# Two-layer trunk on one core: the state product takes one summed operand, and the instruction order is drawn up from other costs

## Chip, cores and metric

The kernel runs on one core of a Trainium2 chip. The time is the device time of one execution in microseconds. TensorE is the matrix engine; VectorE, ScalarE and GpSimd are the other compute engines, and SyncE (SP) issues most transfers. In the profile they are PE (with PEld for its weight loads), DVE, ACT, POOL and SP.

## What is computed

Two residual layers over 256 positions of width 1024, in float32. The first is a state-space mixer, the second an attention:

```python
for i in range(DEPTH):                    # DEPTH = 2
    hn = rms_norm(h, norm_g[i])
    y = s5_mixer(hn, ...) if i % 2 == 0 else moba_mixer(hn, ...)
    h = h + y
# s5_mixer: u, z = split(hn @ w_in); 64 groups of 16 channels and 64 complex states
#   s[t] = a * s[t-1] + f * (B u[t]);  y = Re(C s) + d * u
#   y = gelu(y); y = y * sigmoid(y @ w_glu + b_glu); return (y * silu(z)) @ w_out
# moba_mixer: q, k, v, z = split(hn @ w_in); 8 heads of 128, norm and rotation of q and k
#   causal attention over the one block of 256 keys; return (o * silu(z)) @ w_out
```

## The kernel before

**How the order comes about.** Every engine call is recorded in `add` as an operation with its engine, an estimated cost, and the operations that it has to follow (data, and the reuse of a buffer: a tile with `bufs=n` goes round among n places). Several calls inside `prog.group()` are one operation. `lay` then plays all five engines forward with those costs: whichever engine is free next takes, among its ready operations, the one with the longest remaining way to the end. `order` does so for some rounds, keeps the best way lengths, and the start times of the last pass are the order in which instructions are written out. So each engine's instruction list is fixed ahead of the run, and a wrong cost can put a waiting instruction in front of ready ones. All instructions are issued from one helper line, L355 in the profile, so groups are told apart by tile names.

**Stages.** (1) Eight `u_step`s multiply the rows of x with the first half of the input weights, 512 columns in plain float32 (each such multiplication is two instructions of TensorE). Their order on TensorE is fixed, with `x_turn8` (transposes of x) and `b_turn` among them; `c_turn` (16 transposes of the output matrix C, from the buffer `Y`) is placed freely, with a push of 10000. (2) The states. For each quarter b of 16 groups VectorE makes an input table `X[b]` (`x_table`: six multiplications and additions of 128x512, buffer `X`, three places), and an output table in `Y` (`y_table`). TensorE turns `X[b]` (`x_turn`) and multiplies it with C (`k_table`); from the four results `w_table` makes `W` (buffer `BW`). `ssm_in(b)` brings the input into states; `rotate(b)` on VectorE multiplies with cosines and sines (`EC`, `ES`) into `t1` and `t2` (two places each) and scans along time; `states(b)` rotates back and leaves two addends, `pa` (tile `tb`, two places) and `pc` (tile `t3`; the profile calls t1, t2 and t3 all `t`). `ssm_within(b)` opens the accumulation of the output with `W`, and `ssm_out(b)` adds the product of `Y` with `pa` and then with `pc`, 32 matrix products of 64x64 by 64 for each. ScalarE takes the result out (`ys`), four transposes and a GELU follow. `z_pair` (64 products of 256 columns in all, from tiles `zh` and `zl`) is independent of all that and fills TensorE in between. (3) `glu_tile`: eight output tiles in split precision (`hi` and `lo` parts, three products each), the parts made by ScalarE and VectorE from each weight tile `wr`. (4) The first output product. (5) The attention: six `chunk`s for q, k and v, normed in `qk_chunk` with a power on GpSimd (tiles `sm`, `mhalf`), eight `head`s, the gate and the last output product.

**The transpose of `b_glu`** (`vb`, a part of the same buffer `Y`) stands in the free part behind `c_turn`; the new contents of `Y` have to follow it.

Of the kernel before, what the change touches and what calls it, by code (L numbers as in the profile page):

```python
# [20 lines left out]
F = mybir.dt.float32  # L21
# [50 lines left out]
class Op:  # L72
    __slots__ = ("eng", "calls", "cost", "deps", "nbytes", "i", "table", "columns", "parts", "push", "mode")


class Program:
# [67 lines left out]
    def add(self, handle, eng, method, a, k):  # L144
# [9 lines left out]
        if dma:  # L154
            cost = self.ISSUE[eng]
        elif eng == "PE":
            if method == "transpose":
                cost = 109 if aps[0].shape[0] >= 64 else 30
            else:
                m, c = n(aps[0]), n(aps[1])  # L160
                if aps[0].dtype == FR:
                    cost = 4 + 0.4455 * max(c, 256)
                else:
                    cost = max(4 * c / 2.4 + 2, 109) * m / 128 * aps[0].shape[0] / 128
                    if m == 32:
                        cost = 42
        elif eng == "DVE":
            two = method in ("tensor_tensor", "scalar_tensor_tensor", "tensor_tensor_scan", "tensor_reduce") or psum
            cost = (70 if not psum else 125) + n(aps[0] if method == "tensor_reduce" else out) * (6.4 if method == "reciprocal" else 2.1 if method == "tensor_tensor_scan" else 1.04 if two else 0.53)
        elif eng == "ACT":  # L170
            cost = 95 + 0.83 * n(aps[0]) + (60 if len(aps) > 1 else 0) + (100 if "accum_out" in k else 0)
        else:
            spread = any(not x.ap[-1][0] for x in aps)
            each = {"memset": 0.85, "tensor_scalar": 5.2}.get(method, 1.8 if spread else 2.2)
            cost = 150 + 205 * n(out) if k.get("op") == OP.pow else 60 + n(out) * each
        if self.open is None:
            op = Op()
            op.eng, op.calls, op.cost, op.deps, op.i = eng, [], 0, {}, len(self.ops)
            op.nbytes, op.table, op.columns, op.parts, op.push, op.mode = 0, None, 0, [], self.push, None
# [5 lines left out]
            if dma and eng == "SP" and self.behind is not None:  # L185
                op.deps[self.behind] = -1
            if self.open is not False and self.grouping:
                self.open = op
        else:
            op = self.open  # L190
        op.calls.append((handle, method, a, k))
        op.cost += cost
        if eng == "PE":
            rows, m = aps[0].shape[0], n(aps[0])
            cycles = 2 * rows if method == "transpose" else n(aps[1]) * (1 if aps[0].dtype == FR else 4)
            first = int(aps[0].offset) // int(np.prod(aps[0].tensor.shape[1:]))
            op.mode = rows <= 64, m <= 64
            op.parts.append((first, rows, max(1, 128 // m), cycles * rows / 128))

            op.columns = sum(w / min(side, sum(q[:2] == (f, r) for q in op.parts)) for f, r, side, w in op.parts)  # L200
# [3 lines left out]
        if dma:  # L204
# [26 lines left out]
    grouping, chain, only, behind, push = False, None, None, None, 0  # L231
# [26 lines left out]
    def lay(self, after, way, forth):  # L258
# [10 lines left out]
        table, columns, mode = None, {}, None  # L269
        for _ in ops:  # L270
# [13 lines left out]
            if e == "PE" and forth:  # L284
                left_over, at = cost, t
                while left_over > 0:
                    tick = int(at // TICK)
                    pace = 1 if columns.get(tick - 1, 0) >= BUSY else 2
                    part = min(left_over, ((tick + 1) * TICK - at) / pace + 1e-6)
                    columns[tick] = columns.get(tick, 0) + o.columns * part / cost  # L290
                    left_over -= part
                    at += part * pace
                cost = at - t
            if o.nbytes and e != "POOL":
                t = max(t, hwdge)
                hwdge = t + 480 * len(o.calls)
# [61 lines left out]
RATE = 270  # L358
MODE = 3000
# [5 lines left out]
NUDGES = ()  # L365
# [10 lines left out]
YZ_G = True  # L376
# [8 lines left out]
def body(ctx: ExitStack, tc: tile.TileContext, x, norm_g, w_in1, a_re, a_im, log_dt, b_re, b_im,  # L385
# [41 lines left out]
    plan = []  # L427
# [26 lines left out]
    state = {"load": 0, "split": 16}  # L454
    AHEAD = 4
# [7 lines left out]
    def load_to(n):  # L463
        while state["load"] < min(n, len(plan)):
# [5 lines left out]
            if len(src.ap) == 3:  # L470
                dst = dst.rearrange("p (k n) -> p k n", k=src.ap[1][1])
            SP.dma_start(dst, src)

    def split_part(i, c0, c1):
# [5 lines left out]
        hi, lo = (w[:, c0:c1] for w in whl[i])  # L480
        act(hi, raw[i][:, c0:c1])
        tt(V, lo, raw[i][:, c0:c1], hi.bitcast(F), SUB)
# [101 lines left out]
    V.tensor_copy(vec[:, 0:16], pt[:, 256:272])  # L584
    xT = tile_([128, 8, S], F, name="ah")
# [230 lines left out]
    def k_table(b):  # L816

        p = wide()
        xv = X[b].rearrange("p (r q x) -> p r q x", r=2, q=8)
        with prog.group():  # L820
            for r in range(2):
                for a in range(2):
                    for hh in range(4):
                        for j2 in range(2):
                            o = 512 * j2 + 16 * hh
                            PE.matmul(p[side(a), o:o + 16], xv[side(j2), r, 2 * hh + a], ct_[side(j2), r, 8 * b + 2 * hh + a],
                                      start=(r == 0 and hh == 0), stop=(r == 1), skip_group_check=True)
        kv = lambda t: t[:, 8 * b:8 * b + 8].rearrange("p (h j) c -> p h j c", j=2)
        tt(V, kv(KS), p.rearrange("p (j x) -> p j x", j=2)[:, :, 0:64].rearrange("p j (h c) -> p h j c", c=16), kv(dm), ADD)

    def w_table():
# [3 lines left out]
        for t in (2, 1, 0):  # L835
            ps = [acc(), acc()]
            with prog.group():
                for a in range(2):
                    rows, o = side(a), C_ID + 64 * a + 16 * (3 - t)
                    PE.matmul(ps[a][rows], cst[rows, o:o + 64], kv[rows], start=True, stop=True)  # L840
            for a in range(2):
# [5 lines left out]
    def ssm_in(b):  # L847

        p = wide()
        prog.push = 10000  # L850
# [8 lines left out]
        prog.push = 0  # L859
# [26 lines left out]
    def states(b, t2, p):  # L886
# [10 lines left out]
        tt(V, gm(pc)[:, 1, :, 1:], z[:, 0], es, MUL)  # L897
        PSTS[b] = pa, pc
# [11 lines left out]
    def ssm_within(b):  # L910
# [6 lines left out]
        prog.push = 20000  # L917
# [5 lines left out]
        prog.push = 0  # L923
        return p

    def ssm_out(b, p):
        for i, t in enumerate(PSTS[b]):
            tv = t.rearrange("p (r a h m) -> p r a h m", r=2, a=2, h=4)
            with prog.group():
                for r in range(2):  # L930
                    for h in range(4):
                        for a in range(2):
                            for j2 in range(2):
                                product(p, h, a, j2, tv[side(j2), r, a, h],
                                        Y[side(j2), r, 8 * b + 2 * h + a].rearrange("p k c -> p (k c)"), False, i == 1 and r == 1)
# [14 lines left out]
    def z_pair(m):  # L950
# [9 lines left out]
        act(zz[:, 2 * m:2 * m + 2].rearrange("p a (m s) -> p a s m", s=4), p.rearrange("p (a s m) -> p a s m", a=2, s=4), AF.Silu)  # L960


    with prog.fixed("PE"):
        for k in range(8):
# [3 lines left out]
            if k == 1:  # L968
                b_turn()
    load_to(14)  # L970
    prog.push = 10000
    c_turn()
    prog.push = 0
    pv0 = wide()
    PE.transpose(pv0[:, 0:8], vb, ident[32:40, 32:40])
    V.tensor_copy(vec[:, 16:24], pv0[:, 0:8])
# [65 lines left out]
    for n in range(8):  # L1042
        if YZ_G:
            tt(V, yT[:, n], yT[:, n], zz[:, n], MUL)
        else:
            stt(V, yT[:, n], yT[:, n], 0.5, zz[:, n], MUL, MUL)
# [275 lines left out]
```

## Time and profile before

| what | value |
|---|---|
| median of 3 runs | 293.67 us (291.27 to 294.46) |
| the profiled execution | 293.73 us |
| its span, first to last instruction | 291.9 us |
| TensorE matmul busy, of the span | 280.2 us, 2551 instructions |
| TensorE weight loads busy | 229.0 us, 2551 instructions |
| VectorE busy | 214.9 us, 430 instructions |
| ScalarE busy | 159.1 us, 306 instructions |
| GpSimd busy | 22.7 us, 26 instructions |

The span leaves out 1.8 us that lie around it. Busy times of one engine are shares of the same span. Neighbouring matmuls overlap in the records, so what one takes of TensorE is read from start to start.

### The profile page before, as it was taken

The numbers are of one execution on the slowest core, as the hardware profiler recorded it, in microseconds if no ns is written. First come the engines' busy times: TensorE is split into PE (matmuls) and PEld (weight loads), VectorE is DVE, ScalarE is ACT, GpSimd is POOL, SyncE is SP. The second block draws the span as 40 slices with busy tenths as digits, with TensorE's granted clock in tenths as the row PEclk, the third lists the DMA queues.
The fourth block names the chain that finished last, engine by engine and source line by source line (L and its number), as shares of the span: only waits on it lengthen the run. The fifth ranks groups of instructions, "written<-read, shape, count | busy, mean of one in ns | idle before, by whom it ended". The sixth has DMA issues, their size and how long they took to land.

```text
span 291.9 us, 6324 instructions
## 1 busy us (share of the span) xinstructions
PE 280.2 (96%) x2551; PEld 229.0 (78%) x2551; DVE 214.9 (74%) x430; ACT 159.1 (55%) x306; POOL 22.7 (8%) x26
## 2 busy tenths in 40 slices
PE   8998999999998969999999999899999999999995
PEld 7454458888677859998888888678888799998884
DVE  0959789998958647976439648898679988699603
ACT  2579347377440358766429347557565766585300
POOL 3100013000000000000000014500013100000000
PEclk9999999999999988999999999999999999999999
DMA  5999454882000193876745643565245472434003
GB/s 177 244 331 277 126 161 122 213 227 76 0 2 2 39 271 131 240 216 207 212 137 153 209 149 138 165 201 187 96 138 162 136 214 77 144 120 166 6 0 144
DMA packets 41596, 43.91 MB, mean 150 GB/s; under 512 B 4552, under 2 KB 31136, under 8 KB 41504
## 3 DMA queue, kind: packets, MB, share of 16 engines
q1 hardware_dynamic: 40608, 42.68, 50.2%
q10 hardware_dynamic: 864, 0.82, 0.8%
q8 instruction: 20, 0.33, 0.5%
q14 instruction: 8, 0.07, 0.1%
q0 software_dynamic: 96, 0.02, 0.0%
HBM read 41.41 MB, written 1.05 MB: 145 GB/s over the span
## 4 chain that ended last, share of the span: by engine, by line
PE 73%; DVE 7%; DMA 6%; ACT 5%; issue 4%; POOL 3%; SPq 1%; ACTq 0%; POOLq 0%
PE uz L355 33%; PE acc L355 23%; PE wide L355 17%; DMA zz<-in_x_dram 4%; POOL sm L355 3%; DVE sm L355 2%; DMA wr<-in_attn_w_in_dram 2%; DVE D L355 2%; ACT ES L355 1%; SPq L355 1%; DVE xp L355 1%; DVE zl L355 1%; ACT EC L355 1%; DVE X L355 1%; ACT X L355 1%
## 5 line engine op out<-in xcount | busy, mean ns | idle before, releaser
L355 DVE TENSOR_TENSOR xp<-wr,X 128x1024 fp32r<-128x1024 f32 x28 | 34.0, 1222 | 13.8 <-ACT X L355 13.7
L355 DVE TENSOR_TENSOR zl<-wr,zh 128x1024 fp32r<-128x1024 f32 x28 | 34.1, 1219 | 6.6 <-ACT zh L355 6.5
L355 ACT ACTIVATE zh<-wr 128x1024 fp32r<-128x1024 f32 x28 | 29.4, 1056 | 15.7 <-PE uz L355 7.9
L355 ACT ACTIVATE X<-wr 128x1024 fp32r<-128x1024 f32 x28 | 29.5, 1057 | 14.7 <-PE uz L355 8.1
L355 PE MATMUL uz<-al,zh 128*128 128x256 f32 x96 | 24.5, 349 | 0.0
L355 PEld LDWEIGHTS uz<-al,zh 128*128 128x128 f32 x96 | 17.9, 190 | 2.7 <-issue 0.8
L355 POOL TENSOR_TENSOR sm<-sm,mhalf 128x4 f32<-128x4 f32 x8 | 13.7, 1714 | 50.7 <-DVE sm L355 50.6
L355 PE MATMUL uz<-zh,ah 128*128 128x512 f32 x40 | 17.6, 490 | 0.0
L355 PE MATMUL acc<-zh,ah 128*128 128x512 f32 x40 | 17.6, 484 | 0.0
L355 PE MATMUL uz<-zl,ah 128*128 128x512 f32 x40 | 17.1, 478 | 0.0
L355 PE MATMUL acc<-zl,ah 128*128 128x512 f32 x40 | 17.1, 476 | 0.0
L355 PE MATMUL uz<-al,zl 128*128 128x256 f32 x64 | 16.6, 389 | 0.0
L355 PEld LDWEIGHTS uz<-al,zl 128*128 128x128 f32 x64 | 11.4, 190 | 3.0 <-issue 1.6
L355 DVE TENSOR_TENSOR Y<-acc,Y 128x512 f32<-128x512 f32 x4 | 2.8, 691 | 11.4 <-PE acc L355 11.4
L355 PEld LDWEIGHTS acc<-zl,ah 128*128 128x128 f32 x40 | 7.5, 189 | 4.2 <-issue 3.3
L355 DVE TENSOR_TENSOR tb<-s,yT 128x512 f32<-128x512 f32 x16 | 10.7, 682 | 0.0
L355 ACT ACTIVATE ys<-acc 128x256 f32<-128x256 f32 (+1 forms) x8 | 3.8, 496 | 12.4 <-PE acc L355 12.3
L355 PEld LDWEIGHTS acc<-zh,ah 128*128 128x128 f32 x40 | 7.4, 190 | 3.9 <-issue 2.9
L355 PEld LDWEIGHTS uz<-zl,ah 128*128 128x128 f32 x40 | 7.3, 189 | 3.3 <-issue 2.2
L355 PEld LDWEIGHTS uz<-zh,ah 128*128 128x128 f32 x40 | 7.3, 189 | 3.3 <-issue 2.4
L355 PE MATMUL uz<-X,ah 128*128 128x512 f32 x24 | 9.9, 411 | 0.0
L355 PE MATMUL acc<-X,ah 128*128 128x512 f32 x24 | 9.8, 408 | 0.0
(279 smaller groups left out, 804.8 us busy)
## 6 DMA issues: line engine op xcount, KB each, us to landing
wr<-in_attn_w_in_dram SPq DMA_DIRECT2D x32, 512.0 KB, 4.2
zl<-in_ssm_w_in_dram SPq DMA_DIRECT2D x8, 512.0 KB, 6.8
wr<-in_ssm_w_glu_dram SPq DMA_DIRECT2D x8, 512.0 KB, 6.3
wr<-in_ssm_w_out_dram SPq DMA_DIRECT2D x8, 512.0 KB, 4.3
wr<-in_attn_w_out_dram SPq DMA_DIRECT2D x8, 512.0 KB, 4.3
zh<-in_ssm_w_in_dram SPq DMA_DIRECT2D x7, 512.0 KB, 8.4
zz<-zz SPq DMA_DIRECT2D x8, 128.0 KB, 2.3
Y<-in_x_dram SPq DMA_DIRECT2D x2, 512.0 KB, 5.2
```

What stands on the lines that cost most here:

```text
L355: getattr(handle, method)(*map(self.real, a), **{q: self.real(v) for q, v in k.items()})
```

## The change

The products of `ssm_out` take one operand in place of two: `pa + pc` is formed on VectorE for all four quarters. `X[3]` is placed in `t1`. The transpose of `b_glu` is written ahead of the u steps, and `c_turn` stands in the fixed order of TensorE behind `u_step(5)`. The costs from which the order is drawn up are others: SiLU, GELU, the power on GpSimd, and the small products of TensorE get set lengths (41 ns each in `k_table`, 500 in `w_table`, 31 in `ssm_in`, 32 in `ssm_within`, 31 in `ssm_out`), and the player of the order counts TensorE's instructions in pages of 256, with a time from the moment that a page is asked for until it is there. Eleven random disturbances of the way lengths (`NUDGES`) are applied before the last pass. What else the diff brings (`EARLY`, `LOW_DMA`, `HOLD`, `Z_TANH`) is switched off by its constants.

```diff
-                    if m == 32:
-                        cost = 42
+                    if self.unit:
+                        cost = self.unit
...
-            cost = 95 + 0.83 * n(aps[0]) + (60 if len(aps) > 1 else 0) + (100 if "accum_out" in k else 0)
+            f = a[2] if len(a) > 2 else AF.Copy
+            each = {AF.Silu: 1.57, AF.Gelu_apprx_tanh: 1.36}.get(f, 0.83)
+            cost = 95 + each * n(aps[0]) + (60 if len(aps) > 1 else 0) + (100 if "accum_out" in k else 0)
...
-            cost = 150 + 205 * n(out) if k.get("op") == OP.pow else 60 + n(out) * each
+            cost = 700 + 350 * n(out) if k.get("op") == OP.pow else 60 + n(out) * each
...
+            op.words += 2 if method == "transpose" or aps[0].dtype == FR else 4
...
+        words, landed = 64, {0: 0.0, 1: 0.0}
...
+                page, to = words // 256, words + o.words
+                if (to + 48) // 256 > (words + 48) // 256:
+                    at = t + cost * (((to + 48) // 256 * 256 - 48 - words) / o.words)
+                    landed[(to + 48) // 256 + 1] = at + (3500 if dma < at + 1500 else 6000)
+                if to // 256 > page:
+                    cost += max(0.0, landed.get(page + 1, 0.0) - t - cost * ((page + 1) * 256 - words) / o.words)
+                words = to
...
+EARLY = {}
+XT1 = 3
+HOLD = False
+Z_TANH = ()
+YZ_G = not Z_TANH
+CT = 5
+LOW_DMA = ()
+SUM = (0, 1, 2, 3)
...
-NUDGES = ()
+NUDGES = (1046, 1100, 1127, 1187, 1265, 1346, 1586, 2485, 2533, 2578, 2604)
...
+    PE.transpose(pt[:, 272:280], vb, ident[32:40, 32:40])
+    V.tensor_copy(vec[:, 16:24], pt[:, 272:280])
...
-        X[b] = tmp("X", NX)
+        X[b] = tmp("t1", 2) if b == XT1 else tmp("X", NX)
...
+        prog.unit = 41
...
+                prog.unit = 500
...
+        prog.push, prog.unit = 10000, 31
...
+        prog.push, prog.unit = 20000, 32
...
+        if b in SUM:
+            tt(V, pa, pa, pc, ADD)
+            pc = None
         PSTS[b] = pa, pc
...
-        for i, t in enumerate(PSTS[b]):
-            tv = t.rearrange("p (r a h m) -> p r a h m", r=2, a=2, h=4)
+        parts_ = [t.rearrange("p (r a h m) -> p r a h m", r=2, a=2, h=4) for t in PSTS[b] if t is not None]
+        prog.unit = 31
+        for tv in parts_:
...
+            if k == CT:
+                c_turn()
     load_to(14)
-    prog.push = 10000
-    c_turn()
-    prog.push = 0
...
-    PE.transpose(pv0[:, 0:8], vb, ident[32:40, 32:40])
-    V.tensor_copy(vec[:, 16:24], pv0[:, 0:8])
```

## Rows read from the trace of the kernel before

**Rows 1.** Busy time of each engine in stretches of the span: from and to in us, length, then for each engine busy us and instructions, the granted clock of TensorE (1.00 is full), the busy share of the 16 transfer engines and GB/s.

```profile
28.00:44.00 16.00, 15.85 (x66) 8.51 (x67) 13.11 (x23) 6.39 (x13) 1.08 (x1) 1.00 0.58 156
44.00:104.50 60.50, 59.02 (x1332) 49.19 (x1330) 52.00 (x76) 30.50 (x52) 3.00 (x4) 1.00 0.35 92
104.50:107.40 2.90, 0.01 (x2) 0.00 (x0) 1.63 (x6) 1.28 (x4) 0.00 (x0) 1.00 1.02 284
107.40:111.00 3.60, 3.58 (x18) 3.24 (x19) 0.00 (x0) 2.17 (x6) 0.00 (x0) 0.53 0.93 296
111.00:135.00 24.00, 24.00 (x196) 23.71 (x197) 19.35 (x34) 17.66 (x33) 0.00 (x0) 1.00 0.64 194
180.00:192.00 12.00, 10.63 (x54) 8.09 (x53) 10.80 (x25) 6.75 (x9) 5.30 (x2) 1.00 0.51 160
192.00:291.90 99.90, 96.28 (x590) 84.56 (x588) 73.14 (x168) 53.23 (x112) 5.28 (x4) 1.00 0.41 127
```

**Rows 2.** The chain of work that ended last, 82 to 112 us, in order of time: start us, length us, what; "issue" is time in which the engine waited for nothing that the profile shows.

```profile
93.65 0.94 issue
...
104.51 2.92 issue
107.42 0.33 PE wide L355 x3
```

**Rows 3.** TensorE's instructions in order of time, 90 to 95 us and 101 to 108 us: start us, length us, line, operation, output<-inputs, shapes, count, idle time before.

```profile
90.41 1.16 PE L355 MATMUL acc<-Y,tb 64*64 64x64 f32 x64
91.39 1.11 PE L355 MATMUL acc<-Y,t 64*64 64x64 f32 x64
92.32 1.11 PE L355 MATMUL wide<-Y,tb 64*64 64x64 f32 x64
...
102.47 1.11 PE L355 MATMUL wide<-Y,tb 64*64 64x64 f32 x64
103.41 1.10 PE L355 MATMUL wide<-Y,t 64*64 64x64 f32 x61
```

**Rows 4.** The transfer queues in the stretch 104 to 108 us: queue and kind, packets, MB, share; "instruction" packets carry instructions to an engine.

```profile
q1 hardware_dynamic: 2162, 1.09, 101.8%
q8 instruction: 1, 0.02, 1.9%
```

**Rows 5.** TensorE's instructions in order of time, 24 to 30 us, in the middle of the fifth u step.

```profile
25.27 1.88 PE L355 MATMUL uz<-zh,ah 128*128 128x512 f32 x4
28.15 1.21 PE L355 MATMUL wide<-cst,Y 64*128 64x64 f32 x16 [1.00 <-ACT ah L355]
```

**Rows 6.** VectorE's waits from 20 to 112 us: what it was about to do, what it waited for, us in total, how many, the longest.

```profile
DVE al L355 <- ACT ah L355: 5.8, 2, 4.5
DVE tb L355 <- PE acc L355: 5.3, 3, 3.0
DVE vec L355 <- PE wide L355: 2.8, 1, 2.8
DVE Y L355 <- PE wide L355: 1.7, 2, 1.3
...
DVE X L355 <- PE wide L355: 0.4, 1, 0.4
```

**Rows 7.** Groups of VectorE's instructions from 20 to 112 us by shape: count, busy us and mean ns of one, idle before.

```profile
L355 DVE TENSOR_TENSOR al<-ah,rrow 128x1024 f32<-128x1024 f32 x2 | 2.4, 1217 | 0.0
```

**Rows 8.** VectorE's instructions in order of time at the transposed `b_glu`, at `X[3]`, at the second rotation, and around the last two `states`: the `TENSOR_SCALAR` rows write the first column of `pa` once TensorE has run `ssm_within`.

```profile
37.58 0.17 DVE L355 COPY vec<-wide 128x8 f32<-128x8 f32 x1 [2.76 <-PE wide L355]
...
46.13 1.66 DVE L355 TENSOR_TENSOR X<-s,yT 128x512 f32<-128x512 f32 x2 [0.41 <-PE wide L355]
...
65.87 1.21 DVE L355 TENSOR_TENSOR t<-wide,EC 128x1024 f32<-128x1024 f32 x1
...
91.64 1.21 DVE L355 TENSOR_TENSOR tb<-t,EC 128x1008 f32<-128x1008 f32 x1 [0.81 <-PE acc L355]
...
96.60 0.19 DVE L355 TENSOR_SCALAR tb<-acc 128x16 f32<-128x16 f32 x1 [1.45 <-PE acc L355]
...
98.75 0.19 DVE L355 TENSOR_SCALAR tb<-wide 128x16 f32<-128x16 f32 x1 [0.79 <-PE wide L355]
```

**Rows 9.** TensorE's instructions in order of time, 64 to 73 us: the last `k_table`.

```profile
69.19 1.27 PE L355 MATMUL wide<-yT,X 64*64 64x16 f32 x58
```

**Rows 10.** TensorE's waits in the whole span: what it was about to do, what it waited for, us in total, how many, the longest.

```profile
PE wide L355 <- issue: 3.9, 2, 2.9
PE wide L355 <- DVE D L355: 1.4, 3, 0.7
...
PE wide L355 <- ACT ah L355: 1.0, 1, 1.0
PE wide L355 <- DVE Y L355: 0.3, 1, 0.3
PE acc L355 <- DVE vec L355: 0.3, 1, 0.3
PE uz L355 <- ACT um L355: 0.2, 1, 0.2
```

**Rows 11.** The chain that ended last from 174 to 192 us: the power on GpSimd in the norm of q and k.

```profile
174.11 1.02 POOL sm L355
...
184.84 3.19 POOL sm L355
```

More of the change, by code (lines that the diff above doesn't have):

```diff
@@ L72 @@
 class Op:
-    __slots__ = ("eng", "calls", "cost", "deps", "nbytes", "i", "table", "columns", "parts", "push", "mode")
+    __slots__ = ("words", "eng", "calls", "cost", "deps", "nbytes", "i", "table", "columns", "parts", "push", "mode")
 class Program:
@@ L184, in add @@
                 self.chain[eng] = op.i
-            if dma and eng == "SP" and self.behind is not None:
-                op.deps[self.behind] = -1
+            if dma and eng == "SP":
+                for j in (self.behind, self.late):
+                    if j is not None:
+                        op.deps[j] = -1
             if self.open is not False and self.grouping:
@@ L203, in add @@
             op.table = {AF.Silu: 0, AF.Sin: 0, AF.Gelu_apprx_tanh: 1, AF.Exp: 2}.get(f)
-        if dma:
+        if dma and "accum_op" in k:
+            op.nbytes = int(np.prod(out.shape)) * 8
+        elif dma:
             run = out.ap[-1][1] if len(aps[0].ap) > 1 else 1
@@ L230, in add @@
             self.seen[name] = keep
-    grouping, chain, only, behind, push = False, None, None, None, 0
+    grouping, chain, only, behind, push, unit, late = False, None, None, None, 0, 0, None
     @contextmanager
@@ L375 @@
 EV_G = ()
-YZ_G = True
 YL_G = ()
@@ L454, in body @@
     state = {"load": 0, "split": 16}
+    last_out = []
     AHEAD = 4
@@ L471, in load_to @@
                 dst = dst.rearrange("p (k n) -> p k n", k=src.ap[1][1])
+            prog.late = last_out[0] if i >= 20 and last_out else None
             SP.dma_start(dst, src)
+            prog.late = None
     def split_part(i, c0, c1):
@@ L480, in split_part @@
         hi, lo = (w[:, c0:c1] for w in whl[i])
+        prog.push = EARLY.get(i, 0)
         act(hi, raw[i][:, c0:c1])
-        tt(V, lo, raw[i][:, c0:c1], hi.bitcast(F), SUB)
+        if i in LOW_DMA:
+            act(lo, hi.bitcast(F), AF.Copy, scale=-1.0)
+            G.dma_start(lo.rearrange("p (k n) -> p k n", k=8), plan[i], accum_op=ADD)
+        else:
+            tt(V, lo, raw[i][:, c0:c1], hi.bitcast(F), SUB)
+        prog.push = 0
     def split_to(n):
@@ L840, in w_table @@
                     PE.matmul(ps[a][rows], cst[rows, o:o + 64], kv[rows], start=True, stop=True)
+            prog.unit = 0
             for a in range(2):
@@ L934, in ssm_out @@
                                 product(p, h, a, j2, tv[side(j2), r, a, h],
-                                        Y[side(j2), r, 8 * b + 2 * h + a].rearrange("p k c -> p (k c)"), False, i == 1 and r == 1)
+                                        Y[side(j2), r, 8 * b + 2 * h + a].rearrange("p k c -> p (k c)"), False,
+                                        tv is parts_[-1] and r == 1)
+        if HOLD:
+            last_out[:] = [len(prog.ops) - 1]
+        prog.unit = 0
         ys = tile_([128, 4, 8, 16], F, name="ys", bufs=2)
@@ L959, in z_pair @@
                           start=(k == 0), stop=(k == 7))
-        act(zz[:, 2 * m:2 * m + 2].rearrange("p a (m s) -> p a s m", s=4), p.rearrange("p (a s m) -> p a s m", a=2, s=4), AF.Silu)
+        zo, zi = zz[:, 2 * m:2 * m + 2].rearrange("p a (m s) -> p a s m", s=4), p.rearrange("p (a s m) -> p a s m", a=2, s=4)
+        if m in Z_TANH:
+            for q in range(2):
+                act(zo[:, q], zi[:, q], AF.Tanh, scale=0.5)
+                stt(V, zo[:, q], zo[:, q], 1.0, zi[:, q], ADD, MUL)
+        else:
+            act(zo, zi, AF.Silu)
     with prog.fixed("PE"):
@@ L969, in body @@
                 b_turn()
+            if k == CT:
+                c_turn()
     load_to(14)
-    prog.push = 10000
-    c_turn()
-    prog.push = 0
+    if CT > 7:
+        prog.push = 10000
+        c_turn()
+        prog.push = 0
     pv0 = wide()
-    PE.transpose(pv0[:, 0:8], vb, ident[32:40, 32:40])
-    V.tensor_copy(vec[:, 16:24], pv0[:, 0:8])
     for i in range(2):
```

9 lines of the change are left out of this document (5 added, 4 removed).

## Prediction, made before the changed kernel was run

> **What bounds the kernel now.** I read the stretches first [rows 1]. From 111 us to the end TensorE's busy time fills nearly every stretch (24.00 of 24.00, 96.28 of 99.90, of which the last 3.3 us are the way out), and the exception, 180 to 192 us, lacks 1.4 us. So the second half is bound by TensorE, and nothing there is taken away. The state stage, 44 to 104.5 us, is busy for 59.02 of 60.50 on TensorE and for 52.00 on VectorE: TensorE bounds it, VectorE is close behind. Right after it come 2.90 us in which TensorE does nothing, and 3.60 us in which it is busy with a granted clock of 0.53, that is mostly at the lower of its two levels, 1.2 GHz. Then the chain [rows 2]: the stage's two holes, 0.94 and 2.92 us, are put down to "issue", so no engine and no data is named. The waits of TensorE [rows 10] show that all others together (1.4, 1.0, 0.3, 0.3, 0.2 us) are smaller than these 3.9. Last, TensorE's order in time [rows 3] shows where the holes stand: inside `ssm_out`, in the run of 64x64 products from `t`, the second addend.
>
> That the holes are instructions that have not arrived is an inference. For it: they cut one group of like instructions in two, and in the window of the longer one the queue that carries instructions moved one packet while ordinary transfers filled the transfer engines (101.8%) [rows 4].
>
> **The change, part by part.** All is counted against the profiled execution, 293.73 us (291.9 of span and 1.8 around it), which stands at the median of the three runs, 293.67.
>
> *a. Products removed.* One addend fewer makes 4 times 32 products, 64 instructions each time, 256 in all. From start to start 64 of them take 91.39 - 90.41 = 0.98, 92.32 - 91.39 = 0.93 and 103.41 - 102.47 = 0.94 us [rows 3]. They lie on the bound engine, and I take 4 x 0.94 = 3.8 us off, with no less than 0 if VectorE takes over (below).
>
> The Trainium skill, "TensorE: Matmul & The Clock Gate", section "Wait — 56ns, not 53.3ns?", says that start to start never falls below about 25 ns however small the product is. The rows have 14.7 ns here, four 64x64 corners being used in turn, so the measurement decides. By the page the 256 instructions would be worth 6.4 us as an estimate and the sum would come to 282.1.
>
> *b. The holes.* Half of the packed instructions of `ssm_out` go, and the new order counts TensorE's instructions in pages, so that slow `z_pair` products can be put between packed groups. Together the holes are 0.94 + 2.92 = 3.86 us. They return between nothing and all of that; I take 3.0, since what follows `ssm_out(3)` is still packed with little left to put between.
>
> *c. The clock.* What ran from 107.4 to 111.0 at 0.53 would take 3.6 x 0.53 = 1.9 us at full clock: 1.7 us. The fall came right behind the long hole; before it, packed small products ran at 1.00 all through the state stage. So it should go with the hole, between 0 and 1.7 (and a loss of the same size if another hole takes its place); I take 1.2.
>
> *d. `c_turn` behind `u_step(5)`.* In the fifth u step TensorE waits 1.00 us for ScalarE's `ah` before the transposes of C [rows 5]. Their 1.13 us (28.15 to the next start at 29.28) are the same elsewhere. In their new place the four remaining products of step 4 and the eight of step 5 stand ahead (12 x 0.47 = 5.6 us, by the four that take 1.88 from 25.27), and ScalarE is done by then. The output tables wait for `c_turn`: VectorE wrote its first `Y` behind a wait that ended at 37.6 [rows 8], and the new place is over by 27.2 + 5.6 + 1.1 = about 34, so nothing is late. 1.0 us off, bounds 0 and 1.0, the whole wait. The transpose of `b_glu`, now early, can hold the first u step if its small transfer is late: 0 to 0.3 by the like wait for `vec` [rows 10]; I take nothing.
>
> *e. Four sums on VectorE.* The nearest row is a 128x1024 addition of float32: 1217 ns [rows 7], so 4 x 1.22 = 4.9 us. A sum can start once the first column of `pa` is there, which VectorE writes after `ssm_within(b)` [rows 8]. Until now the product with `tb` could start before `t` was ready; now it can't. Sums 0 to 2 have `z_pair` and other quarters' products as cover on TensorE. The last one has the first tiles of the next stage at best. I take one sum on the path, 1.2 us, bounds 0 and 4.9. Behind a waiting sum in VectorE's list stand the next quarter's rotation and the splits of the gate weights, for which in turn the next weight transfers wait.
>
> *f. `X[3]` in `t1`, `Y` free earlier.* VectorE stands 2.8 us for the transposed `b_glu` (with it `Y` comes free) and 0.4 us for the place of `X[3]` [rows 6, 8]. Both go. TensorE's holes that follow from them are 0.3 and 0.2 us [rows 10]: 0.5 off. The 3.2 us of VectorE pay for most of the sums, and that is why I don't take more in e.
>
> *g. The order of the rest.* Nothing is removed there. GpSimd's power takes 1.02 us once and 3.19 another time [rows 11]; its old cost was 150 + 205 x 4 = 970 ns, the new one is 700 + 350 x 4 = 2100, so transposes that wait for it should be put later. TensorE lacks 1.4 us in 180 to 192 [rows 1]. I take 0.7 off; a new order can as well lose what it gains, so the bounds are 2.0 off and 2.0 on.
>
> Sum: 293.7 - 3.8 - 3.0 - 1.2 - 1.0 + 1.2 - 0.5 - 0.7 = **284.7**. With every term at its good end it would be about 280.
>
> **The rivals.**
>
> *VectorE becomes the bound of the states.* Its 52.0 us from 44 to 104.5 [rows 1] grow by 4.9 and lose the 2.8 that can be done before 44: 54.1. If its present waits (60.5 - 52.0 = 8.5 us) all stay, since TensorE's order makes them, the stage takes 62.6, 2.1 longer. With the long hole, the clock, d and g as above, 293.7 + 2.1 - 2.9 - 1.2 - 1.0 - 0.7 = 290.0. For it: 5.3 us of its waits are for TensorE's `acc`, which the change doesn't touch. Against: the long holes of VectorE come late (5.8 us for `ah`), where the sums are already done. Chance 0.13, half of it within 1%.
>
> *The holes stay.* If instructions are not late, or the new order meets full transfers again at the same point, b and c are nothing: 293.7 - 3.8 - 1.0 + 1.2 - 0.5 - 0.7 = 288.9. For it: the splits that free weight tiles stand next to `ssm_out` also in the new kernel, so transfers start there, and they ran at 284 GB/s through the long hole [rows 1]. Against: half the packed instructions. Chance 0.12. The Trainium skill, "Runtime: NRT & Kernel Launch", section "Instruction fetch mechanics", says that fetching is hidden since instructions are issued more slowly than they arrive; by it this rival would be the forecast. The two cuts inside one group of products speak against the page.
>
> *Slower: `X[3]` keeps a place of `t1`.* `t1` has two places, and the second rotation needs the one in which `X[3]` lies until `k_table(3)` has read it. Before, the last `k_table` started at 69.2 and ended about 70.5, and the second rotation started at 65.9 [rows 8, 9]. If TensorE's order leaves it there, VectorE stands 4.6 us with all of its list behind it, and the sums (4.9) are no longer hidden: 293.7 + 4.6 + 4.9 - 2.8 - 0.4 - 1.0 = 299.0. It decides from the point at which `k_table(3)` ends more than about 2 us behind the end of the first rotation. Against: `X[3]` is now made some 10 us earlier (it was taken up again at 46.1 [rows 8]), so its readers can run before the first rotation. Chance 0.08.
>
> *The costs don't describe the chip.* The new order is drawn up for set lengths; if the second half loses the 2 us of g twice over, and a alone remains of the rest, 293.7 - 3.8 - 1.0 + 1.2 + 1.0 = 291. Chance 0.05.
>
> **How the numbers follow.** The forecast has 0.62, its own range is 280 to 288: the ends of b, c and g. 290.5 takes in the holes' rival and half of VectorE's; the slower one and the last are left out, and below 280 there is nothing to gain. A measurement of this kernel can tell about 1% from no change, 2.9 us. Faster by more than that (below 290.7): 0.62 + 0.12 + half of 0.13 + some of the last, 0.82. Within 1%: 0.10. Slower: the third rival, 0.08.
>
> **What would show it.** TensorE's instructions fall by 256 to 2295, and no group from `Y` and `t` is left; VectorE has four new instructions of 1.2 us from `tb` and `t`. Right for b and c: no wait "issue" over 0.5 us on TensorE, and a granted clock of 1.00 through the whole gelu stretch. Right for d: no wait for `ah` in front of the transposes of C. Right for e and f: VectorE's wait for `vec` is gone and its waits on `acc` don't grow; the first rotation's `t` follows `k_table(3)` closely. Right as a whole: the first full tile of the gate product starts at about 102 in place of 111, and the rest keeps its 180 us. Wrong: if TensorE has holes named after VectorE between `ssm_in` and `ssm_out`; if the hole moves with a packed group; if the second half is longer than before by more than 2 us.

## The result and the profile after

The changed kernel takes **283.34 us** (median of 4 runs, 282.56 to 285.17), beside 294.06 for the kernel before on the same chip: a ratio of 0.966, with a 95% interval of 0.958 to 0.974. The forecast was 284.7. The profiled execution took 283.35 us, of which 281.6 are span.

The page of the changed kernel, its busy times and the slices of the granted clock:

```profile
PE 272.7 (97%) x2295; PEld 223.2 (79%) x2295; DVE 219.9 (78%) x434; ACT 159.0 (56%) x306; POOL 20.2 (7%) x26
...
PEclk9999999999999999999999999999999999999999
```

TensorE has 256 instructions less, and no slice of its clock is below 0.9 of full speed. VectorE's 434 instructions are the 430 of before and four sums. The stretches, cut where the stages lie now; the columns are those of [rows 1]:

```profile
98.50:102.60 4.10, 2.89 (x123) 2.44 (x113) 3.30 (x5) 4.07 (x9) 0.00 (x0) 1.00 0.86 233
102.60:126.40 23.80, 23.78 (x200) 23.41 (x198) 19.25 (x36) 17.52 (x35) 0.00 (x0) 1.00 0.73 237
...
44.00:102.60 58.60, 56.49 (x1085) 46.02 (x1083) 54.11 (x77) 32.72 (x57) 3.45 (x4) 1.00 0.42 111
...
149.45:278.20 128.75, 128.75 (x749) 111.81 (x747) 100.11 (x219) 73.40 (x141) 11.37 (x9) 1.00 0.45 142
```

The state stage ends at 102.6 and not at 107.4 to 111 [rows 1]. The attention, from its first chunk to the last product, is busy on TensorE for all of its 128.75 us; before, the same stretch was 131.87 long and busy for 130.18:

```profile
156.73:288.60 131.87, 130.18 (x749) 111.59 (x747) 99.29 (x220) 73.28 (x141) 14.42 (x9) 1.00 0.45 138
```

TensorE's waits in the whole span, in the form of [rows 10]:

```profile
PE wide L370 <- ACT rrow L370: 1.3, 1, 1.3
...
PE wide L370 <- DVE Y L370: 0.8, 2, 0.6
PE wide L370 <- issue: 0.6, 1, 0.6
```

The two holes of 3.9 us are gone, and so are the waits for `D` in the attention. But there are new ones, and TensorE's order in time says where they stand (columns as in [rows 3]):

```profile
31.61 1.22 PE L370 MATMUL wide<-cst,Y 64*128 64x64 f32 x16
...
37.01 0.40 PE L370 MATMUL wide<-cst,s 128*128 128x128 f32 x2 [0.55 <-issue]
...
40.01 1.09 PE L370 MATMUL wide<-cst,X 128*128 128x128 f32 x8 [1.29 <-ACT rrow L370]
...
98.05 1.16 PE L370 MATMUL acc<-Y,tb 64*64 64x64 f32 x64
99.14 0.66 PE L370 MATMUL uz<-cst,ys 128*128 128x128 f32 x4
100.16 1.16 PE L370 MATMUL wide<-Y,tb 64*64 64x64 f32 x64 [0.35 <-DVE tb L370]
102.17 0.66 PE L370 MATMUL uz<-cst,ys 128*128 128x128 f32 x4 [0.86 <-ACT ys L370]
102.59 0.37 PE L370 MATMUL wide<-ah,zh 128*128 128x256 f32 x1
```

The transposes of C (31.61) start without a wait, where 1.00 us stood in [rows 5]. The one "issue" of 0.55 us is in the u steps, not in a packed group; its cause stays open. At the end of the states 0.35 us remain for the last sum, and 0.86 for ScalarE's last `ys`. VectorE's four sums, and what is left from 20 to 103 us of its 5.3 us of waits for `acc` [rows 6]:

```profile
L370 DVE TENSOR_TENSOR tb<-tb,t 128x1024 f32<-128x1024 f32 x4 | 4.8, 1218 | 0.0
```

```profile
DVE tb L370 <- PE acc L370: 0.7, 2, 0.4
```

**Where the time went**, by the starts of the same products in the two timelines of TensorE: the first output product, the first product of the first chunk and the last product of all, before and after.

```profile
133.65 0.40 PE L355 MATMUL acc<-X,U 128*128 128x512 f32 x1
156.73 0.47 PE L355 MATMUL acc<-X,ah 128*128 128x512 f32 x1
288.27 0.28 PE L355 MATMUL wide<-zh,BW 128*128 128x256 f32 x1
```

```profile
126.36 0.40 PE L370 MATMUL acc<-X,U 128*128 128x512 f32 x1
149.45 0.48 PE L370 MATMUL acc<-X,ah 128*128 128x512 f32 x1
277.93 0.28 PE L370 MATMUL wide<-zh,BW 128*128 128x256 f32 x1
```

The first output product starts 7.29 us earlier. From there to the first chunk both take 23.1. From the first chunk to the end of TensorE's work the change takes off another 3.06. Together TensorE's work ends 10.34 us earlier, and the span is 10.3 shorter.

### The profile page after: what moved, and what is told of

Its sections match the earlier page's. It is cut to its first block, busy times and chain, and to the rows that moved or that the text cites. A ratio compares the mean times of both kernels' runs of the same rounds, so it can differ in the third digit from the quotient of the medians.

```text
span 281.6 us, 5813 instructions
## 1 busy us (share of the span) xinstructions
PE 272.7 (97%) x2295; PEld 223.2 (79%) x2295; DVE 219.9 (78%) x434; ACT 159.0 (56%) x306; POOL 20.2 (7%) x26
## 4 chain that ended last, share of the span: by engine, by line
PE 74%; DMA 8%; DVE 6%; ACT 6%; SPq 4%; issue 1%; DVEq 0%; ACTq 0%
PE uz L370 35%; PE acc L370 26%; PE wide L370 13%; SPq L370 4%; DMA zz<-in_x_dram 3%; DVE X L370 3%; DMA qkg<-in_attn_q_gain_dram 2%; DMA zh<-in_ssm_w_in_dram 2%; DVE tb L370 2%; DMA zz<-zz 1%; ACT zz L370 1%; ACT yT L370 1%; ACT ES L370 1%; ACT EC L370 1%; DVE t L370 1%
## 5 line engine op out<-in xcount | busy, mean ns | idle before, releaser
L370 PE MATMUL uz<-al,zh 128*128 128x256 f32 x96 | 25.1, 352 | 0.0
L370 PE MATMUL uz<-al,zl 128*128 128x256 f32 x64 | 15.8, 384 | 0.0
L370 POOL TENSOR_TENSOR sm<-sm,mhalf 128x4 f32<-128x4 f32 x8 | 10.7, 1333 | 48.9 <-DVE sm L370 48.9
L370 ACT ACTIVATE zz<-uz 128x512 f32<-128x512 f32 x4 | 4.6, 1140 | 9.3 <-PE uz L370 9.3
L370 PE MATMUL acc<-zh,al 128*128 128x512 f32 x24 | 9.5, 395 | 0.0
L370 PE MATMUL uz<-zh,al 128*128 128x512 f32 x24 | 9.5, 395 | 0.0
```

Source lines behind the costliest of these rows:

```text
L370: getattr(handle, method)(*map(self.real, a), **{q: self.real(v) for q, v in k.items()})
```

## The experiments

All times are medians. The kernel before ran on the same chip each time; the ratio to it, with its 95% interval, is worked out from the single runs, so it need not be the quotient of the two medians.

| kernel | us | runs | before, us | ratio, 95% |
|---|---|---|---|---|
| changed | 283.34 | 4 | 294.06 | 0.966 [0.958, 0.974] |
| sums alone, order of before | 291.18 | 10 | 293.49 | 0.996 [0.991, 1.001] |
| order alone, no sums | 292.15 | 10 | 293.49 | 0.994 [0.990, 0.999] |
| no disturbances | 286.30 | 4 | 293.49 | 0.976 [0.969, 0.983] |
| old cost of the power | 286.78 | 4 | 293.49 | 0.978 [0.971, 0.985] |
| before, new cost of the power | 291.10 | 1 | 292.58 | one run |
| no pages in the player | 283.84 | 3 | 292.58 | 0.971 [0.967, 0.975] |
| sums twice as dear | 288.22 | 3 | 292.58 | 0.986 [0.978, 0.993] |
| `rt` and splits behind the last sum | 283.15 | 6 | 293.60 | 0.968 [0.962, 0.973] |
| and `rrow` first | 283.35 | 6 | 293.60 | 0.968 [0.963, 0.973] |
| `X[3]` in `X` | 284.98 | 4 | 293.60 | 0.974 [0.967, 0.981] |
| table loaded early | 286.99 | 6 | 293.44 | 0.976 [0.972, 0.980] |

**1. The sums alone.** Every engine's order stays that of before; the sum is issued behind the last instruction of `states`, and the second addend's products are left out of the list.

```diff
+        for made, products, call in self.sums:
+            last = max(made, key=lambda i: place[i])
...
+            self.ops[last].calls.append(call)
+            for i in products[1:]:
+                self.ops[i].calls.clear()
```

> The kernel before in its own order, unchanged, but for the sums: each addition stands behind the last step of its states and the product with the second addend is left out. If the products cost what the rows said (256 instructions, 3.8 us) and the holes come from instructions that arrive late, TensorE loses 3.8 us of work and at least the short hole, and one sum of 1.2 us comes on the path: 287 to 290. If VectorE's four additions eat what TensorE gains and the order is what counts, 292 to 295.

It is 2.3 us faster than before, if it is faster at all, and lies between the two ranges that were expected. No "issue" is left. TensorE's longest wait and the stretch behind it:

```profile
PE acc L364 <- DVE tb L364: 2.6, 1, 2.6
```

```profile
99.46:102.88 3.42, 3.42 (x34) 2.55 (x35) 3.42 (x4) 1.34 (x2) 0.00 (x0) 0.50 0.03 10
```

The holes of before are filled with a wait for the sum, and it is dear twice: 2.6 us, and behind it 3.4 us at a granted clock of 0.50 (the lower of the two levels, 1.2 GHz), just as behind the long hole of before. In the old order VectorE gets to the sum too late, and most of what TensorE saves is lost in waiting for it.

**2. The order alone.** The changed kernel without the sums.

```diff
-SUM = (0, 1, 2, 3)
+SUM = ()
```

> The changed kernel with two addends again (no sums), its order drawn up anew with all its new costs and places. If the sum is worth its products and half of the packed instructions, 3.8 us and some 1 to 3 us of holes come back: 288 to 291. If the new order alone makes the gain, 283 to 285.

292.15, 1.3 us off and slower than either range that was expected; "issue" is back with 3.2 us in four pieces, though this order counts pages. One piece of 0.7 us stands in the u steps, like the 0.55 of the changed kernel; the other three stand in packed groups. TensorE's order in time at two of them:

```profile
94.76 1.11 PE L370 MATMUL wide<-Y,tb 64*64 64x64 f32 x64
95.69 0.40 PE L370 MATMUL wide<-Y,t 64*64 64x64 f32 x13
97.04 0.97 PE L370 MATMUL wide<-Y,t 64*64 64x64 f32 x50 [0.94 <-issue]
...
107.44 1.08 PE L370 MATMUL wide<-Y,t 64*64 64x64 f32 x57
109.88 0.34 PE L370 MATMUL wide<-Y,t 64*64 64x64 f32 x7 [1.35 <-issue]
```

Again one group of like products is cut in two. So it is the sums, which halve the packed instructions, that take the holes away. The parts alone give 2.3 and 1.3 us, together 10.7. The starts of the first output product (133.65 before) tell more: with the sums alone it starts at 130.82, 2.8 us earlier; with the order alone at 135.04, 1.4 us later; with both 7.3 earlier. What the order alone gains it gains in the attention (128.61 us in place of 131.82; experiment 6 has the cause). Ahead of the attention, then, the sums need another order and that order needs the sums. The eleven disturbances fall on other operations when the list of operations changes, and experiment 5 shows that they matter, so a part of the 1.4 us may be theirs.

**3. Packed products by themselves.** To see what "issue" is, a kernel of its own: nothing of the computation is kept. TensorE multiplies 64x64 corners that lie ready from the start, 768 products without transfers and 768 while 28 weight tiles are loaded, each time between slow products.

```python
            for m in range(n):
                for a in range(2):
                    for j in range(2):
                        o = 64 * (m % 8)
                        PE.matmul(p[a][side(j), o:o + 64], x8[side(a), a, o:o + 64], x8[side(a), j, 512 + o:576 + o], start=True, stop=True, skip_group_check=True)
...
        packed(p[0:2], 192)
```

> No part of the computation is kept: 768 packed products of 64x64 by 64 on four corners run back to back, once with no transfers and once while 28 weight tiles are fetched; x is copied to the output. If the holes come from instructions that arrive late, the run of 14.7 ns per instruction breaks about every 128 matmuls (256 instructions with the weight loads), in the quiet half by 1 to 2 us each time, in the loaded half by 2 to 4 us; the halves last about 30 to 45 and 45 to 70 us. If instructions always arrive in time, both run through in 768 x 2 x 14.7 ns = 22.6 us.

One run, 165.3 us. TensorE's order in time, first in the quiet half, then in the loaded one:

```profile
20.80 3.02 PE L355 MATMUL p<-x 64*64 64x64 f32 x191
25.22 2.09 PE L355 MATMUL p<-x 64*64 64x64 f32 x128 [1.39 <-issue]
28.67 2.09 PE L355 MATMUL p<-x 64*64 64x64 f32 x128 [1.36 <-issue]
...
39.31 2.09 PE L355 MATMUL p<-x 64*64 64x64 f32 x128 [1.64 <-issue]
...
94.33 3.36 PE L355 MATMUL p<-x 64*64 64x64 f32 x128 [4.32 <-issue]
99.43 2.09 PE L355 MATMUL p<-x 64*64 64x64 f32 x128 [1.74 <-issue]
104.53 3.38 PE L355 MATMUL p<-x 64*64 64x64 f32 x128 [3.01 <-issue]
111.27 3.42 PE L355 MATMUL p<-x 64*64 64x64 f32 x128 [3.36 <-issue]
```

The two halves in the view of stretches (there is no ScalarE column here), and the queue of instructions in the first:

```profile
20.80:61.70 40.90, 25.06 (x1537) 23.49 (x1536) 0.00 (x0) 0.00 (x0) 1.00 0.02 5
85.90:141.90 56.00, 31.75 (x1538) 30.22 (x1537) 0.00 (x0) 0.00 (x0) 0.82 0.71 257
```

```profile
q8 instruction: 12, 0.20, 2.0%
```

With nothing to wait for, the group breaks at every 128 matmuls, that is with their weight loads at every 256 instructions, and one packet of instructions is moved for each: 12 packets, 1536 matmuls and 1536 loads. Both halves last as long as expected for instructions that arrive late (40.9 and 56.0 us), but the idle times of the loaded half spread wider than the 2 to 4 us expected. From break to break it takes 3.45 us (25.22 to 28.67) to 3.73, and the 256 instructions run in 2.09 of them. While weights are loaded, the time from break to break grows to 5.10 and 6.74 us; in a part of it the clock is lower, and the same instructions run for 3.4 us.

That this is what the holes of before are, the times of the instruction packets in the traces show. Alone, TensorE starts again 1.22 to 1.61 us behind the end of a packet, in all 21 breaks. In the kernel before the packets of the two holes end at 93.26 and 105.95, and TensorE starts again at 94.59 and 107.42, 1.34 and 1.47 us later; in the three packed holes of experiment 2 it is 0.99 to 1.52. Between the two restarts of before lie 769 instructions of TensorE and of its weight loads, three times 256 and one. The holes fit the rows: [rows 3] have three groups of 64 in one run and a fourth that the hole cuts, and the longer hole falls into the full transfers of [rows 4]. In the changed kernel the groups at the end stand alone, with transposes between them. The 0.55 us of "issue" in its u steps come 12 us behind a packet and are not of this kind.

The fall of the clock is seen behind the long hole of before and in this loaded half. It doesn't follow every hole: the quiet half, with its idle 1.36 to 1.64 us, runs at 1.00 throughout, and so does the profiled execution of experiment 2.

The Trainium skill, "Runtime: NRT & Kernel Launch", section "Instruction fetch mechanics", says that instructions come in blocks of 256, which these rows show, and that fetching them is mostly hidden. For packed 64x64 products the rows say otherwise: 1.36 of 3.45 us are idle, or 1.64 of 3.73.

**4. The player without pages.** Is the counting of pages needed?

```diff
-                if to // 256 > page:
+                if False:
```

> The changed kernel whose order is drawn up without the pages of instructions (the late arrival costs nothing in the drawing). If half the packed instructions is what closes the holes, the order can do without: 283 to 285, no issue hole over 1 us. If counting pages closes them, holes of 1 to 3 us named issue come back between the states: 285 to 288.

283.84, no "issue" at all. The order barely needs the pages once the sums halve the packed groups.

**5. The disturbances of the way lengths.**

```diff
-NUDGES = (1046, 1100, 1127, 1187, 1265, 1346, 1586, 2485, 2533, 2578, 2604)
+NUDGES = ()
```

> The changed kernel without the eleven random disturbances of the way lengths. If the gain is in the removed work and in costs that fit, the order is nearly as good: 283 to 286. If the disturbances carry it, 288 or more.

286.30, just above the range for an order that is nearly as good, and 3.0 us more than the changed kernel; the intervals of the ratios overlap a little, the spans differ by 2.9 (284.5 and 281.6). TensorE at a `k_table`, and the stretch behind it:

```profile
47.72 2.42 PE L370 MATMUL wide<-yT,X 64*64 64x16 f32 x64 [1.48 <-DVE Y L370]
```

```profile
47.65:54.48 6.83, 6.76 (x80) 6.14 (x81) 6.83 (x13) 3.20 (x6) 0.00 (x0) 0.50 0.74 190
```

A wait of 1.48 us for an output table comes with 6.8 us at the lower clock. The other three executions have a mean clock of 0.985 to 0.994, where those of the changed kernel have 0.999 to 1.000. What the disturbances bring is an order that happens to avoid this.

**6. The cost of the power, both ways.** The changed kernel with the old cost, and the kernel before with the new one.

```diff
-            cost = 700 + 350 * n(out) if k.get("op") == OP.pow else 60 + n(out) * each
+            cost = 150 + 205 * n(out) if k.get("op") == OP.pow else 60 + n(out) * each
```

> The changed kernel with the old cost of GpSimd's power (970 ns for four values in place of 2100). If that cost is why TensorE no longer waits in the norm of q and k, the waits come back behind 150 us, 2 to 3 us in all: 285.5 to 286.5, with the stretch up to the first output product as in the changed kernel. If not, 283 to 284 and no wait there.

> The kernel before with the new cost of GpSimd's power alone, its order drawn up anew. If that cost makes TensorE wait in the norm of q and k, the part from the first chunk to TensorE's end (131.8 us before, 128.8 changed) shortens by 2 to 3 us, and the time is 290.5 to 292, with the holes named issue as before. If not, that part stays at 131 to 132.

With the old cost the whole takes 286.78, 3.4 us more than the changed kernel and a little above the expected range, and the attention takes 131.44 us from its first chunk to the end (128.76 in the changed kernel), and the three waits for `D`, 1.4 us, are back. With the new cost in the kernel before it takes 128.73 in place of 131.82, while 3.6 us of "issue" stay in the states; 291.10 beside 292.58 agrees, in one run. So one constant makes the whole gain of the second half. Two of the waits in the kernel before, each with the product ahead of it, and behind them the same place with the new cost:

```profile
185.10 0.40 PE L355 MATMUL acc<-zh,al 128*128 128x512 f32 x1
186.17 0.63 PE L355 MATMUL wide<-cst,D 128*128 128x128 f32 x4 [0.67 <-DVE D L355]
...
189.90 0.40 PE L355 MATMUL acc<-X,al 128*128 128x512 f32 x1
190.88 0.63 PE L355 MATMUL wide<-cst,D 128*128 128x128 f32 x4 [0.58 <-DVE D L355]
```

```profile
185.96 0.40 PE L355 MATMUL acc<-zh,al 128*128 128x512 f32 x1
186.19 0.60 PE L355 MATMUL wide<-cst,D 128*128 128x128 f32 x4
```

A product is followed after 0.23 us where nothing waits. The two holes are therefore 1.07 - 0.23 = 0.84 and 0.98 - 0.23 = 0.75, and not the 0.67 and 0.58 in brackets: the modelled end of the last product hides 0.17 of each. Read in this way five holes in the attention of before come to 2.5 us, and the wait list shows 1.4.

**7. More work on VectorE.** One more 128x1024 instruction, the maximum of `pc` with itself, stands ahead of each sum and changes no value.

```diff
+            prog.ops[-1].calls.insert(0, (nc.vector, "tensor_tensor", (), dict(out=pc, in0=pc, in1=pc, op=MAX)))
```

> The changed kernel in its own order, with a second operation of the same size on VectorE ahead of each sum (the larger of t and t, which changes nothing): 4 x 1.2 = 4.9 us more on VectorE. If one or two sums are on the path, 1.2 to 2.4 us more, 284.5 to 286. If VectorE bounds the states, 4.9 more: 287.5 to 289. If the sums are hidden, 283 to 284.

288.22, 4.9 us more for 4.9 us of work, though its three runs spread from 286.58 to 289.78; the spans of the profiled executions differ by 4.8 (286.4 and 281.6). Two of TensorE's waits are new or grown:

```profile
PE acc L370 <- DVE tb L370: 2.6, 1, 2.6
PE wide L370 <- DVE tb L370: 1.9, 1, 1.9
```

So in this order VectorE has no room left for more work ahead of the sums.

**8. Less work on VectorE ahead of the last sum.** The order of the changed kernel is kept, but eight rotation tables (`rt`, 0.9 us) and the weight splits that stood ahead of the last sums go behind them.

```diff
+        pairs += [(m["sum"][3], i) for i in m["rt"]]
+        pairs += [(m["sum"][3], m["split"][i]) for i in (17, 18, 19)]
```

> The changed kernel in its own order, but for VectorE's list: the eight small products for rt (with the 1.3 us that they wait for a transfer) and the two splits zl that stand between the last steps of the states are put behind the last sum. 1.0 + 1.3 + 2.4 = 4.7 us go from ahead of the last sum. If VectorE bounds the states, so that each us ahead of the sums counts in full, 279 to 281.5 (the splits are wanted right after). If TensorE bounds them, within 1 us of the changed kernel, 282.5 to 284.

283.15, no difference that can be told. VectorE ends the last sum at 97.1, in the changed kernel at 100.1; the wait for `tb` is gone, and TensorE then waits 1.24 for `ys`. ScalarE's order in time ahead of it:

```profile
96.58 1.13 ACT L389 ACTIVATE zz<-uz 128x512 f32<-128x512 f32 x1 [3.44 <-PE uz L389]
97.74 1.28 ACT L389 ACT_TABLE_LOAD   x1
...
99.94 0.44 ACT L389 ACTIVATE ys<-acc 128x256 f32<-128x256 f32 x1
```

Of the three microseconds on VectorE little comes through, since ScalarE is next: it waits for the last `z_pair`, loads the table of the GELU (1.28 us) and only then comes to `ys`. In the profiled execution the first output product starts at 125.22 in place of 126.36, 1.1 us earlier, and the medians differ by 0.2. VectorE bounds the states in one direction: more of its work costs in full, and of the 3 us less no more than 1.1 come back.

**9. And the wait for `rrow`.** As 8, with the copy of `rrow` ahead of the sines on ScalarE.

```diff
+        pairs += [(m["rrow"], i) for i in m["turn"] if place[i] > place[m["rrow"]] - 40]
```

> The same, and on ScalarE the copy of rrow stands ahead of four steps of the sines, so that TensorE's wait of 1.3 us for it in the last u step goes. If VectorE bounds what follows, no more than 0.5 us less than without this; if TensorE does, 1.0 to 1.3 less.

283.35. The 1.3 us for `rrow` are gone, and a wait for VectorE's `Y` has grown to 1.1, with a granted clock of 0.50 from 48.3 to 51.7 us. The hole moved and was not closed.

**10. `X[3]` back in `X`.**

```diff
-XT1 = 3
+XT1 = None
```

> The changed kernel with the last input table in the three places of X again, its order drawn up anew. If the place was worth what the prediction took for it (0.5 us, with VectorE's wait of 0.4 back), 283.5 to 284.5; if VectorE bounds the states, its wait for the first k_table comes back in full, 1 to 4 us: 284.5 to 287.5.

284.98, 1.6 us more than the changed kernel, with intervals that overlap; the spans differ by as much (283.2 and 281.6). VectorE's longest wait from 20 us to the end of the states is now 2.9 us, for ScalarE's `yT` ahead of an output table, and TensorE waits 1.0 for `U` and 0.8 for `um`. The order is drawn up anew with the place, but with the same eleven disturbances; that they suit it as well is not shown, so the 1.6 us are the place and the order together.

**11. The table loaded early.** On top of 8: a GELU of one column ahead of the last `z_pair`'s gate loads the table in ScalarE's idle time, and that gate becomes z (1 + tanh(z/2)) / 2, with the product on VectorE.

```diff
+        o.calls[:] = [(silu, "activation", (zo, zi, AF.Tanh), dict(scale=0.5)),
+                      *[(vector, "scalar_tensor_tensor", (zo[:, q], zo[:, q], 1.0, zi[:, q]), dict(op0=ADD, op1=MUL)) for q in range(2)]]
+        scalar[n - 1].calls.append((silu, "activation", (tiny, tiny, AF.Gelu_apprx_tanh), {}))
```

> Base is the order with the rt splits behind the last sum (283.15 us), where the sum ends 3 us earlier and nothing is gained because TensorE then waits 1.2 us for ScalarE's ys, whose chain is SiLU (waiting 3.4 us for TensorE), ACT_TABLE_LOAD 1.28 us, GELU, ys. Edit: a GELU of one column directly ahead of the last z_pair's gate on ScalarE, so that the table is loaded in the idle time there; that gate as z * (1 + tanh(z/2)) with the tanh on ScalarE and the product in two instructions on VectorE, the factor 0.5 in the two later multiplications. Theory 'ScalarE's table load is what is late behind the sums': the wait for ys goes, ssm_out's end to the first gate tile closes by 1.0 to 1.3 us, 282.0. Rival 'the chain of transposes and splits behind ys is as late on VectorE': the table load moves, the wait is renamed to VectorE, 283.0 to 283.5. Nothing of the computation is left out.

286.99, 3.8 us slower than 8, which neither theory gave. The load does move: `ys` starts at 98.35 and not at 99.94. But the two products on VectorE wait for the tanh in front of the last sum. VectorE's order in time there, and TensorE's:

```profile
97.69 1.14 DVE L398 SCALAR_TENSOR_TENSOR zz<-zz,uz 128x256 f32<-128x256 f32 x2 [2.04 <-ACT zz L398]
...
99.03 1.23 DVE L398 TENSOR_TENSOR tb<-tb,t 128x1024 f32<-128x1024 f32 x1
```

```profile
104.86 0.58 PE L398 MATMUL wide<-al,zh 128*128 128x256 f32 x1 [2.69 <-DVE al L398]
```

The last sum ends at 100.3, 3.1 us later than in 8; the tables and weight splits behind it, and with them the first gate operand `al`, are late, TensorE stands 2.69 us, and runs at a clock of 0.50 from 104.86 to 110.5. Whether the early load alone would give the 1.2 us, with those two products behind the sum, stays open.

## Why the prediction was right, point by point

The span was forecast 9.0 us shorter and is 10.3 shorter. The terms:

| term | forecast (bounds), us | in the traces |
|---|---|---|
| a products removed | -3.8 | about -4.0, see below |
| b holes "issue" | -3.0 (-3.86 to 0) | -3.9 |
| c clock | -1.2 (-1.7 to 0, or a loss) | -1.7 |
| d `c_turn`, early `b_glu` | -1.0 (-1.0 to 0), and 0 (0 to 0.3) | -1.0, and +0.3 for `vec` |
| e sums on VectorE | +1.2 (0 to 4.9) | +0.35, and +0.86 for `ys` |
| f `X[3]`, `Y` free earlier | -0.5 | -0.5, and +0.8 for two waits for `Y` |
| g rest of the order | -0.7 (-2.0 to 2.0) | -3.1 |
| no term | | +1.3 for `rrow`, +0.55 "issue", -0.4 warm-up products |

*a* can't be read by itself. TensorE's busy time up to the first output product falls from 126.91 to 120.81 us; of these 6.1 us the clock is 1.7 and the shorter warm-up 0.4, which leaves an estimate of 4.0.

*b* holds, and its inference, that the holes are instructions that have not arrived, is now shown by experiments 2 and 3. The second ground of the term is not: page counting wasn't needed (experiment 4). Halving the packed instructions was enough, and the holes went in full, so the 0.86 that the forecast kept back for `ssm_out(3)` was too careful. By the forecast's own sign, no "issue" over 0.5 us, the 0.55 in the u steps is a narrow miss, but it is no packed hole.

*c* holds for the two profiled executions. It is less firm than it looks: of 46 executions of the kernel before that ran beside the experiments, 15 have a mean granted clock of 0.998 or more (median 292.3 us), 24 have 0.993 or 0.994 (293.3) and 7 have 0.988 (294.4). The order of the instructions is the same in all of them, so the clock doesn't fall each time; a fall of the size of c, 1.7 of 291.9 us, is a mean of 0.994.

*d* names the right wait, and the hole of 1.00 went. The 1.29 us for `rrow` that came within 9 us of the new place are not its price: experiments 2, 5 and 10 have `c_turn` at the same place and no such wait. ScalarE's copy of `rrow` stands behind sines, for which it had waited 8.5 us for VectorE's `ES`. The forecast had no term for what ScalarE has to do for TensorE's next work.

*e* comes to 1.2 by luck. Only 0.35 us are a wait for the last sum. The 0.86 for `ys` are ScalarE's chain: with the sum done 3 us earlier (experiment 8) that wait is 1.24. Its reason is only half right, too. "The 3.2 us of VectorE pay for most of the sums" would mean room on VectorE; experiment 7 finds none for more, since 4.9 us more cost 4.9. That the sums are paid by the new order and by those 3.2 us together is argued: in the order of before the same sums make a wait of 2.6 (experiment 1).

*f*: the wait for `vec` behind the transpose is gone from VectorE's list, as forecast. The forecast put the 0.2 us for ScalarE's `um` to this term, and no row ties `um` to `X[3]`. It took only TensorE's holes in the trace of before, and not what the longer list of VectorE would have made of them; by experiment 10 the place of `X[3]`, with the order that goes with it, is worth some 1.6 and not 0.5.

*g* is the term that failed, outside its bounds: 3.06 where 0.7 was taken and 2.0 was the end. Experiment 6 gives its cause, the power's cost alone. The mechanism was named; the size was half of a wait list that itself showed 1.4 of 2.5 us.

So the total came out nearer than its terms: a, b, c, g and the warm-up gave some 4.3 us more than was taken, and waits that had no term, or a smaller one, took 2.9 back.

**The rivals.** VectorE's busy time to the end of the states is 54.11 us, as its rival had it (54.1), but it ends at 102.6 all the same: its waits for `acc` fell from 5.3 to 0.7 us, which the rival had left as they were. The holes' rival is what experiment 2 looks like in the states, but for the clock, which stays at 1.00 there. `X[3]` passed its rival's point: `k_table(3)`, now from `t`, ends at 64.4, 3.7 us behind the last scan of the first rotation (60.7), where the forecast had put the point at about 2. It isn't slower all the same, since VectorE has the rotation back of the first quarter, a weight split and small multiplications, with a wait of 1.27 us for a transfer, in between: the second rotation starts at 66.4, and with no wait for `t`'s place. The sum of the last rival doesn't follow its words: it says that a alone remains, but takes off d as well, and has 1.0 where twice the 2 us of g would be 4. With a, e and 4 us it would be 295. The costs describe the chip better than was allowed for.

## What to carry to other kernels

A long run of small products can be bound by the arrival of its own instructions, as the 64x64 products are here: where "issue" cuts a group of like products in two, count instructions, not columns, and look for a way to have fewer of them. Read a hole from start to start against the same pair without a wait, before its list of waits is taken for its price. And when work moves to an engine that is nearly full, price it in both directions: what more of it costs need not be what less of it gives back.

## What had not been expected of the hardware

A run of 64x64 products breaks at every 256 instructions even with idle transfer queues: 3.45 to 3.73 us from break to break against 2.09 us of work, and up to 6.74 us while weights are loaded, with TensorE starting again 1.22 to 1.61 us behind the end of the packet that brings the instructions. And the granted clock can make a small wait dear: behind a hole of 1.48 us it was 0.50 for 6.8 us, which by an estimate (half of 6.8) costs 3.4 us. Which holes it follows is not settled here: it followed this one, and none of the 1.36 to 1.64 us in the quiet half of experiment 3.
